# A decoder trunk on one core: thirty weight splits taken into the first feed-forward layer and kept in DRAM, layer norm additions on VectorE, conv taps loaded earlier and divided anew

## The chip, the core and the metric

The kernel runs on one core of a Trainium2 chip. A core has a matrix engine (TensorE, in the profile PE, with the loading of its weights as PEld), three engines for elementwise work (VectorE or DVE, ScalarE or ACT, GpSimd or POOL), and SyncE (SP), from whose queue nearly all transfers between DRAM and the on-chip memory are issued. Each engine works through its own instructions in order; semaphores tie them together. The metric is the device time of one execution in microseconds. Three runs of the kernel before gave 1237.91 to 1237.98, median 1237.97 us.

## The reference

The input is a sequence of 512 positions of 1024 features in float32. Two layers follow one another; each is a mixer and a feed-forward part, each with a scaled residual and a layer norm.

```python
for layer in range(DEPTH):                       # DEPTH = 2
    if layer % 2 == 0:                           # layer 0: state space group and attention group
        h = x @ mix_w_in[i] + mix_b_in[i]
        u, q, k, v = jnp.split(h, ...)
        mix = jnp.concatenate([s5_out, sb_out], axis=-1) @ mix_w_out[i] + mix_b_out[i]
    else:                                        # layer 1: conformer convolution
        mix = conformer_conv(x, conv_w_pw1[i], ...)
    x = layer_norm(DEEPNORM_ALPHA * x + mix, ln1_g[layer], ln1_b[layer])
    ffn = jnp.square(jax.nn.relu(x @ w1 + b1)) @ w2 + b2          # 1024 -> 4096 -> 1024
    x = layer_norm(DEEPNORM_ALPHA * x + ffn, ln2_g[layer], ln2_b[layer])

def conformer_conv(x, w_pw1, b_pw1, w_dw, b_dw, ln_g, ln_b, w_pw2, b_pw2):
    h = x @ w_pw1 + b_pw1                        # 1024 -> 2048
    val, gate = jnp.split(h, 2, axis=-1)
    h = val * jax.nn.sigmoid(gate)
    h = depthwise_causal_conv(h, w_dw) + b_dw    # 31 taps for each of 1024 channels
    h = jax.nn.silu(layer_norm(h, ln_g, ln_b))
    return h @ w_pw2 + b_pw2                     # 1024 -> 1024
```

## The kernel before

Features lie on the 128 partitions and positions along the free axis, so an activation is eight tiles of 128 x 512. All products are made at more than the precision of one pass: a matrix is split into a high part rounded to the type fp32r and the low rest, and a product is three passes, high by high, high by low and low by high (`gemm`, L199 to L208; its matmuls are on L207). Activations and weights are both split: `split` (L196) for activations, class `Weights` for weights.

**Weights.** `Weights` (L53 to L109) holds a list of units in the order of use. A unit is 8 x 128 rows by 128 columns, 512 KB in float32. `fetch` (L65) loads the chunk that a unit lies in, mostly 1 MB for two units, from SP's queue into one of two raw buffers. `_prep` (L77) then makes the parts: ACT casts the raw unit to the high part (L90) and DVE subtracts to get the low part (L91), both into one of eight slots in turn. `next` hands out the next unit and has the units up to five ahead prepared first. A slot is free again when PE has read its unit for the last time. Around a layer norm the splits can be held behind it by `fence`.

**Order of the work.** After the mixer of layer 0 come, in this order (chunks of the trace in brackets):

- `tail_norm_lead("a")`: the rest of the output product of the mixer ("tail", tiles tla, in two halves of 256 positions), the layer norm, and the first six products of the feed-forward part ("lead", tiles fl).
- The feed-forward part of layer 0 in four blocks of eight hidden tiles. `ffn1` makes the hidden tiles (f), `accum` adds their products to X (acf). For a block of eight, `accum` takes a unit for each of its eight columns. The last block's second product is the tail of the next step.
- The load of the 31 x 1024 conv taps in two pieces (L982), eight transposes on PE (L985) and their split on DVE (wdw, wdh, wdl).
- `tail_norm_lead("b")`: tail tlb, the layer norm and four lead products (pl), the first two tiles of the pointwise product of the convolution.
- The convolution. For each of the eight channel tiles `glu_tile` makes value and gate (pv, pg), their product hp and its split (hph, hpl); `taps_pe` gives some of the 31 taps to PE, each as a diagonal matrix that ACT makes in two parts (dh, dl; L1030 holds the matmuls, into cv); `taps_dve` gives two taps to ACT and the others to DVE (L339, two running sums cy and cz), and adds the sums and cv. `PE_TAPS` says how many taps of each tile PE takes, first for the whole tile or its first half, then for second halves. The last two tiles are worked in halves (tiles 6 and 7). Then comes the layer norm of the convolution for the first half, and for the second.
- `tail_norm_lead("d")`: the second pointwise product (tld), layer norm, six lead products for layer 1's feed-forward part (fl). `residual` rebuilds X from the split parts on POOL.
- The feed-forward part of layer 1 (f, g, h) and the final norm. Its weights follow the same unit order.

**The layer norm** (class `LN`) runs by halves. `add` sums the eight tiles as they come: the first six additions of a half on POOL, the last on DVE (L833). `colmean` (L841) is a product with a matrix of 1/1024 that gives the mean (mp...) and the variance (vp...). In `norm`, DVE subtracts the mean, ACT squares, POOL adds the squares of four tiles in a chain of three (L853), DVE adds those of the other four, and the variance product takes the two sums. `others` names products of PE that are issued ahead of the mean's and the variance's.

The order of instructions on an engine is made from the order in the code and a cost model of the framework, which lets later work move up where it judges earlier work not ready.

Of the kernel before, what the change touches and what calls it, by code (L numbers as in the profile page):

```python
# [16 lines left out]
P = 128  # L17
# [35 lines left out]
class Weights:  # L53


    def __init__(self, tc, ahead):
        self.tc, self.nc, self.ahead = tc, tc.nc, ahead
        self.slots, self.units, self.raw, self.urgent, self.fence, self.hold = [], [], None, True, None, False
        self.done, self.got, self.chunk, self.ready = 0, 0, {}, {}
# [17 lines left out]
    def _prep(self, n):  # L77
        nc = self.nc
        while self.done < min(n, len(self.units)):
            key, src, nk, ncol, off, width = self.units[self.done]  # L80
            self.fetch(self.done)
# [14 lines left out]
            self.done += 1  # L96

# [50 lines left out]
def kernel(ctx: ExitStack, tc: tile.TileContext, a: dict, out: bass.AP):  # L148
# [610 lines left out]
    def accum(nps, xk, name, ncol, first=True, cols=((0, T),)):  # L759
# [3 lines left out]
        for c0, c1 in cols:  # L763
            for j in range(KT):
# [7 lines left out]
                else:  # L772
                    tt(x, x, ps[:, c0:c1], ALU.add)

# [26 lines left out]
    units = units_of("mo", w_out, 4, 4, range(0, D, 256), 512)  # L801
    for layer in range(2):
        if layer:
            for j in range(0, D, 128):
                units += units_of("pw1", a["conv_w_pw1"][0], 0, 8, [j], 256)
                units += units_of("pw1", a["conv_w_pw1"][0], 0, 8, [D + j], 256)
            units += units_of("pw2", a["conv_w_pw2"][0], 0, 8, range(0, D, 128), 256)
        k0 = 0
        for nb in FFN_BLOCKS[layer]:
            units += units_of(f"f1{layer}", a["ffn_w1"][layer], 0, 8, range(k0 * P, (k0 + nb) * P, 128), 256)  # L810
            if layer == 0:
                units += units_of("f20", a["ffn_w2"][0], k0, nb, range(0, D, 1024 // nb), 256 if nb == 8 else 512)
# [9 lines left out]
    class LN:  # L822
# [5 lines left out]
        def add(self, j, ys, c0, c1):  # L828
# [3 lines left out]
            if j:  # L832
                (V if j == KT - 1 else G).tensor_tensor(self.s[c0], ys[0][:, c0:c1] if j == 1 else self.s[c0], ys[j][:, c0:c1], op=ALU.add)  # L833
# [10 lines left out]
        def norm(self, ys, c0, c1, others=(None, None)):  # L844
# [67 lines left out]
    class Lead:  # L912
# [35 lines left out]
    def ffn1(layer, bi, k0, nb, xs, fps, first=()):  # L948
        hs = []
        for i in range(nb):  # L950
# [12 lines left out]
            hs.append((hh, hl))  # L963
        return hs
# [7 lines left out]
    xs, first = tail_norm_lead(cat[4:8], "a", rb[0], ("ln1_g", 0), ("ln1_b", 0), LEAD, "fl0")  # L972
    k0 = 0
    for bi, nb in enumerate(FFN_BLOCKS[0]):
        hs = ffn1(0, bi, k0, nb, xs, nps, first if bi == 0 else ())
        if bi < len(FFN_BLOCKS[0]) - 1:
            accum(nps, hs, f"f0{bi}", 1024 // nb, bi == 0)
        k0 += nb
    wdw = hid.tile([P, KT, CONV], F32, tag="wdw", name="wdw")
    for f in range(2):  # L980
        wn = tmp(f"wn{f}")[:CONV]
        nc.sync.dma_start(wn, a["conv_w_dw"][0][:, f * T : (f + 1) * T])  # L982
        ps = stp(f"wd{f}")
        for i in range(4):
            PE.transpose(ps[:, i * 32 : i * 32 + CONV], wn[:, i * P : (i + 1) * P], ident[:CONV, :CONV])  # L985
        V.tensor_copy(wdw[:, 4 * f : 4 * f + 4, :], ps[:, :P].rearrange("p (i t) -> p i t", t=32)[:, :, :CONV])
    wdh = hid.tile([P, KT, CONV], F32R, tag="wdh", name="wdh")
    wdl = hid.tile([P, KT, CONV], F32, tag="wdl", name="wdl")
    V.tensor_copy(wdh, wdw)
# [211 lines left out]
```

## Time and profile before

| | us |
|---|---|
| median of three runs | 1237.97 |
| profiled execution | 1239.18 |
| its span (first to last instruction) | 1237.4 |
| PE busy | 1195.6 (97%) |
| DVE busy | 779.3 (63%) |
| ACT busy | 567.1 (46%) |
| POOL busy | 107.1 (9%) |

The page gives, for each engine, the time that its instructions cover, and a row of 40 digits, one for each fortieth of the span (31 us), with the busy share in tenths. PE's instructions overlap in the pipeline, so that a PE row of nines isn't proof that PE did as much as it can; the chain of waits and the gaps between PE's instructions say more. The chain that ended last runs through PE for 75% of the span, DVE for 16%, ACT 4%, DMA 3%. A row of a group reads: line, engine, operation, output and inputs by their names, shapes, count, then busy time in us and the mean of one in ns, then the idle time of the engine before them and who ended it.

### The profile page before, as it was taken

The numbers are of one execution on the slowest core, as the hardware profiler recorded it, in microseconds if no ns is written. First come the engines' busy times: TensorE is split into PE (matmuls) and PEld (weight loads), VectorE is DVE, ScalarE is ACT, GpSimd is POOL, SyncE is SP. The second block draws the span as 40 slices with busy tenths as digits, with TensorE's granted clock in tenths as the row PEclk, the third lists the DMA queues.
The fourth block names the chain that finished last, engine by engine and source line by source line (L and its number), as shares of the span: only waits on it lengthen the run. The fifth ranks groups of instructions, "written<-read, shape, count | busy, mean of one in ns | idle before, by whom it ended". The sixth has DMA issues, their size and how long they took to land.

```text
span 1237.4 us, 16678 instructions
## 1 busy us (share of the span) xinstructions
PE 1195.6 (97%) x6559; PEld 1015.3 (82%) x6559; DVE 779.3 (63%) x1321; ACT 567.1 (46%) x1020; POOL 107.1 (9%) x145
## 2 busy tenths in 40 slices
PE   9899999999999999999999999699899999999997
PEld 7776777789888888888998889689898888888885
DVE  8998774578633434434398999999853443434446
ACT  7736575635523324224255766876562332323230
POOL 1001100131000000000140011123400000000000
PEclk9999999999999999999999999889899999999999
DMA  8510141241533223333133121012052232423211
GB/s 206 162 37 20 35 119 52 85 137 42 163 102 102 80 90 102 102 102 98 43 103 103 35 69 35 1 48 90 33 172 69 85 119 68 134 68 105 86 51 68
DMA packets 111662, 105.93 MB, mean 86 GB/s; under 512 B 9378, under 2 KB 99746, under 8 KB 111584
## 3 DMA queue, kind: packets, MB, share of 16 engines
q1 hardware_dynamic: 111424, 104.84, 27.0%
q8 instruction: 51, 0.84, 0.3%
q14 instruction: 27, 0.22, 0.1%
q10 hardware_dynamic: 160, 0.03, 0.0%
HBM read 100.66 MB, written 4.19 MB: 85 GB/s over the span
## 4 chain that ended last, share of the span: by engine, by line
PE 75%; DVE 16%; ACT 4%; DMA 3%; issue 2%; POOL 1%; DVEq 0%; SPq 0%; ACTq 0%; POOLq 0%
PE f L207 23%; PE g L1131 12%; PE acf L207 11%; PE fl L207 4%; PE h L1115 3%; PE tld L207 3%; DVE cz L339 3%; PE tlb L207 2%; PE cv L1030 2%; DVE wlo L91 2%; DVE cy L339 2%; PE pl L207 1%; PE pv L207 1%; PE pg L207 1%; DVE X L339 1%
## 5 line engine op out<-in xcount | busy, mean ns | idle before, releaser
L90 ACT CAST whi<-raw 128x1024 fp32r<-128x1024 f32 x176 | 183.9, 1049 | 396.9 <-PE f L207 112.1
L91 DVE TENSOR_TENSOR wlo<-raw,whi 128x1024 fp32r<-128x1024 f32 x176 | 219.4, 1251 | 221.7 <-ACT whi L90 221.1
L1131 PE MATMUL g<-whi,hh 128*128 128x512 f32 x208 | 81.5, 392 | 0.0
L1131 PE MATMUL g<-wlo,hh 128*128 128x512 f32 x208 | 81.5, 392 | 0.0
L1131 PE MATMUL g<-whi,hl 128*128 128x512 f32 x208 | 81.4, 391 | 0.0
L207 PE MATMUL f<-xdh,whi 128*128 128x512 f32 x208 | 80.9, 389 | 0.0
L207 PE MATMUL f<-xah,whi 128*128 128x512 f32 x208 | 80.9, 389 | 0.0
L207 PE MATMUL f<-xal,whi 128*128 128x512 f32 x208 | 80.9, 389 | 0.0
L207 PE MATMUL f<-xdh,wlo 128*128 128x512 f32 x208 | 80.9, 389 | 0.0
L207 PE MATMUL f<-xdl,whi 128*128 128x512 f32 x208 | 80.9, 389 | 0.0
L207 PE MATMUL f<-xah,wlo 128*128 128x512 f32 x208 | 80.9, 389 | 0.0
L207 PE MATMUL acf<-hl,whi 128*128 128x512 f32 x192 | 75.2, 392 | 0.0
L207 PE MATMUL acf<-hh,whi 128*128 128x512 f32 x192 | 74.9, 390 | 0.0
L207 PE MATMUL acf<-hh,wlo 128*128 128x512 f32 x192 | 74.7, 389 | 0.0
L197 ACT CAST hh<-fr 128x512 fp32r<-128x512 f32 x64 | 39.7, 621 | 71.7 <-DVE fr L335 71.5
L198 DVE TENSOR_TENSOR hl<-fr,hh 128x512 fp32r<-128x512 f32 x64 | 44.2, 691 | 37.3 <-ACT hh L197 37.2
L339 DVE SCALAR_TENSOR_TENSOR cy<-hp,wdw,cy 128x512 f32<-128x512 f32 (+1 forms) x91 | 60.9, 678 | 0.1
L339 DVE SCALAR_TENSOR_TENSOR cz<-hp,wdw,cz 128x512 f32<-128x512 f32 (+1 forms) x86 | 59.9, 700 | 0.0
L1030 PE MATMUL cv<-hph,dh 128*128 128x256 f32 (+1 forms) x113 | 39.9, 353 | 10.0 <-ACT hph L197 8.3
L335 DVE TENSOR_TENSOR fr<-fr 128x512 f32<-128x512 f32 x64 | 43.8, 686 | 5.4 <-ACT fr L136 5.4
L1131 PEld LDWEIGHTS g<-whi,hl 128*128 128x128 f32 x208 | 39.1, 188 | 8.6
L1131 PEld LDWEIGHTS g<-wlo,hh 128*128 128x128 f32 x208 | 39.1, 188 | 8.6
(684 smaller groups left out, 3168.4 us busy)
## 6 DMA issues: line engine op xcount, KB each, us to landing
raw<-in_ffn_w_dram SPq DMA_DIRECT2D x48, 1024.0 KB, 5.4
raw<-in_ffn_w_dram SPq DMA_DIRECT2D x32, 512.0 KB, 3.5
raw<-in_conv_w_pw_dram SPq DMA_DIRECT2D x12, 1024.0 KB, 5.4
raw<-in_mix_w_in_dram SPq DMA_DIRECT2D x16, 512.0 KB, 4.0
xin<-in_x_dram SPq DMA_DIRECT2D x8, 256.0 KB, 4.1
raw<-in_s_w_glu_dram SPq DMA_DIRECT2D x4, 512.0 KB
raw<-in_mix_w_out_dram SPq DMA_DIRECT2D x4, 512.0 KB
raw<-in_mix_w_out_dram SPq DMA_DIRECT2D x2, 1024.0 KB
```

The lines of the kernel that those rows point to most:

```text
L90: i0 = nc.scalar.copy(hi, raw).ins
L91: i1 = nc.vector.tensor_sub(lo, raw, hi.bitcast(F32)).ins
L197: i0 = S.copy(hi, src).ins
L198: i1 = V.tensor_sub(lo, src, hi.bitcast(F32)).ins
L207: ins = PE.matmul(ps[:, c0:c1], u[:, k, ksl], v[:, c0:c1], start=start and k == 0 and i == 0, stop=stop and k == n - 1 and i == 2).ins
L335: V.tensor_tensor(o, x, y, op=op)
L339: V.scalar_tensor_tensor(o, x, s, y, op0=op0, op1=op1)
L1030: PE.matmul(cps[j][:, c0:c1], u, v[:, t + c0 : t + c1], start=t == 0 and i == 0, stop=t == n - 1 and i == 2)
L1115: PE.matmul(ps, u, v, start=k == 0 and i == 0, stop=k == nk - 1 and i == 2)
L1131: PE.matmul(pss[b], u, v[:, kk, :], start=k + kk == 0 and i == 0, stop=k + kk == nb - 1 and i == 2)
```

## The change

The change has six parts.

1. *Thirty units are split early and kept.* The 16 units of the first pointwise product (pw1), the 8 of the second (pw2) and the first 6 of layer 1's feed-forward part (f1l) get entries among the units of layer 0's feed-forward part: two after each group of four hidden tiles from tile 8 on, and two and four after the fourth and the eighth column of the first three `accum` calls. `keep` takes such a unit, split as any other, and writes both parts to DRAM from SP's queue, 512 KB each. In layer 1 these units are of the kind "split": `_prep` loads both parts from DRAM into the slot by POOL's queue, and makes no cast and no subtraction for them, and the fence doesn't hold them.
2. *The additions of the layer norms a, b, c and d* are all on DVE. The squares are added in four pairs on DVE, and the variance product takes four sources in place of two.
3. *The taps are loaded before block 1 of layer 0's feed-forward part*, with their transposes and split, and not before tail b.
4. *PE_TAPS* is changed; for the last two tiles the second half on PE is done for tile 7 before tile 6 (`TAIL`).
5. *The second halves of the first two of layer 1's lead products* are made together, input tile by input tile (`TOGETHER`).
6. *The residual's eight additions* in layer 1 are on DVE.

```diff
-PE_TAPS = ((5, 8, 10, 10, 9, 11, 17, 16), (10, 10, 10, 10, 10, 10, 13, 14))
+PE_TAPS = ((2, 6, 8, 9, 11, 14, 13, 14), (10, 10, 10, 10, 10, 10, 13, 8))
+TAIL = "P60 P70 V60 V70 G61 G71 N0 P71 P61 V61 V71 N1".split()
-GLU_FIRST = True
+TOGETHER = {'fl1': 2}
+LN_ON_V = "abcd"
+KEEP_FROM = 8
...
             key, src, nk, ncol, off, width = self.units[self.done]
+            if key[0] == "split":
+                pool, s = self.slots[self.done % len(self.slots)]
+                w = tuple(pool.tile([P, nk, ncol], F32R, tag=f"w{x}{s}", name=f"w{x}{self.done}", bufs=1) for x in ("hi", "lo"))
+                for x, d in zip(w, self.kept[key[1]]):
+                    nc.gpsimd.dma_start(x, d)
+                self.ready[self.done] = w
+                self.done += 1
+                continue
...
+    def keep(self, i):
+
+        w = self.next()
+        self.kept[i] = tuple(self.tc.dram_tile([P, *w[0].shape[1:]], F32, name=f"kept{x}{i}") for x in "hl")
+        for x, d in zip(w, self.kept[i]):
+            self.nc.sync.dma_start(d, x.bitcast(F32))
...
-                (V if j == KT - 1 else G).tensor_tensor(self.s[c0], ...)
+                (V if j == KT - 1 or self.n in LN_ON_V else G).tensor_tensor(self.s[c0], ...)
...
-            for j in (1, 2, 3):
-                G.tensor_tensor(sq[0], sq[0], sq[j], op=ALU.add)
-            tt(sq[4], sq[4], sq[5], ALU.add)
-            tt(sq[6], sq[6], sq[7], ALU.add)
-            tt(sq[4], sq[4], sq[6], ALU.add)
-            var = self.colmean([sq[0], sq[4]], c0, c1, "v", others[1])
+            for j in range(0, KT, 2):
+                tt(sq[j], sq[j], sq[j + 1], ALU.add)
+            var = self.colmean(sq[::2], c0, c1, "v", others[1])
...
         def finish(self):
             self.run(self.n - len(self.held))
-            for w, ps in self.held:
-                gemm(ps, w, slice(0, P), self.xs, *HALVES[1])
+            n, (c0, c1) = TOGETHER.get(self.name, 0), HALVES[1]
+            for k, (xh, xl) in enumerate(self.xs):
+                for (hi, lo), ps in self.held[:n]:
+                    for i, (u, v) in enumerate(((hi, xh), (hi, xl), (lo, xh))):
+                        PE.matmul(ps[:, c0:c1], u[:, k, :], v[:, c0:c1], start=k == 0 and i == 0, stop=k == KT - 1 and i == 2)
+            for w, ps in self.held[n:]:
+                gemm(ps, w, slice(0, P), self.xs, c0, c1)
...
     for bi, nb in enumerate(FFN_BLOCKS[0]):
+        if bi == 1:
+            taps()
         hs = ffn1(0, bi, k0, nb, xs, nps, first if bi == 0 else ())
...
-            G.tensor_tensor(X[j], xs[j][0].bitcast(F32), xs[j][1].bitcast(F32), op=ALU.add)
+            tt(X[j], xs[j][0].bitcast(F32), xs[j][1].bitcast(F32), ALU.add)
```

More of the change, by code (lines that the diff above doesn't have):

```diff
@@ L757, with accum @@
             glu()
-    def accum(nps, xk, name, ncol, first=True, cols=((0, T),)):
+    def accum(nps, xk, name, ncol, first=True, cols=((0, T),), keep=lambda j: ()):
         nj = ncol // P
@@ L773, in accum @@
                     tt(x, x, ps[:, c0:c1], ALU.add)
+                for k in keep(j):
+                    W.keep(k)
     accum(mm, cat[0:4], "mo", 256)
@@ L801 @@
     units = units_of("mo", w_out, 4, 4, range(0, D, 256), 512)
+    later = []
+    for j in range(0, D, 128):
+        later += units_of("pw1", a["conv_w_pw1"][0], 0, 8, [j], 256)
+        later += units_of("pw1", a["conv_w_pw1"][0], 0, 8, [D + j], 256)
+    later += units_of("pw2", a["conv_w_pw2"][0], 0, 8, range(0, D, 128), 256)
+    later += units_of("f1l", a["ffn_w1"][1], 0, 8, range(0, LEAD * P, 128), 256)
+    kept = [k for j in range(0, 16, 4) for k in (j, j + 2, j + 1, j + 3)] + list(range(16, 24 + LEAD))
+    keep_at, n = {}, 0
     for layer in range(2):
         if layer:
[L804 to L807, printed above, removed]
+            units += [(("split", i), None, 8, 128, 0, 0) for i in range(24 + LEAD)]
         k0 = 0
         for nb in FFN_BLOCKS[layer]:
-            units += units_of(f"f1{layer}", a["ffn_w1"][layer], 0, 8, range(k0 * P, (k0 + nb) * P, 128), 256)
+            for m in range(k0, k0 + nb, 4):
+                units += units_of(f"f1{layer}", a["ffn_w1"][layer], 0, 8, range(max(m, LEAD * layer) * P, min(m + 4, k0 + nb) * P, 128), 256)
+                if layer == 0 and m >= KEEP_FROM:
+                    keep_at["f", m + 3] = kept[n : n + 2]
+                    units += [later[i] for i in kept[n : n + 2]]
+                    n += 2
+            for j in range(0, KT, 4) if layer == 0 else ():
+                units += units_of("f20", a["ffn_w2"][0], k0, nb, range(j * P, (j + 4) * P, 128), 256)
+                if k0 + nb < 32:
+                    m = 4 if j else 2
+                    keep_at["a", k0, j + 3] = kept[n : n + m]
+                    units += [later[i] for i in kept[n : n + m]]
+                    n += m
             if layer == 0:
-                units += units_of("f20", a["ffn_w2"][0], k0, nb, range(0, D, 1024 // nb), 256 if nb == 8 else 512)
+                pass
             else:
@@ L963, in ffn1 @@
             hs.append((hh, hl))
+            for k in keep_at.get(("f", m), ()) if layer == 0 else ():
+                W.keep(k)
         return hs
@@ L1067 @@
             ln.add(j, [x and x[0] for x in acc], c0, c1)
[L1068 to L1069 removed]
+    for o in TAIL:
+        j, (c0, c1) = int(o[1]), HALVES[int(o[-1])]
+        if o[0] == "P":
             taps_pe(j, c0, c1)
[L1071 removed]
+        elif o[0] == "V":
             taps_dve(j, c0, c1)
             ln.add(j, [x and x[0] for x in acc], c0, c1)
[L1074 to L1089 removed]
+        elif o[0] == "G":
+            glu_tile(j, H, T)
+        else:
+            ys = [x[0] for x in acc]
+            r = ln.norm(ys, c0, c1)
+            cs_ = cs_ or new_x("cs")
+            for j in range(KT):
+                y = ys[j][:, c0:c1]
+                tt(y, y, r, ALU.mult)
+                act(y, y, AF.Silu, bias=pv("conv_ln_b", j), scale=pv("conv_ln_g", j))
+                done = split(cs_[j][0][:, c0:c1], cs_[j][1][:, c0:c1], y)
+                if c0 == 0 and j == FJ:
+                    W.fence = done
     W.ahead = AHEAD[0]
```

50 lines of the change are left out of this document (16 added, 34 removed).

## The prediction

> **What bounds the kernel now.** I read the page first, for the slices of busy time.
>
> ```profile
> PE   9899999999999999999999999699899999999997
> DVE  8998774578633434434398999999853443434446
> ```
>
> PE is nearly full everywhere, so only stretches in which PE waits can be shortened. DVE is full in slices 1 to 4 and again in 20 to 29, the tail of layer 0's feed-forward, the convolution and the tail behind it. The change acts there and in the feed-forward before it (slices 11 to 19, PE 9, DVE 3 to 5). Next I asked for busy time by stage, with the borders put at events of the chain of waits.
>
> ```profile
> 330.00:592.00 262.00, 262.00 (x1153) 216.07 (x1153) 106.45 (x121) 79.36 (x97) 0.00 (x0) 1.00 0.30 97
> 592.00:666.60 74.60, 73.37 (x598) 71.73 (x596) 49.59 (x97) 32.69 (x63) 17.90 (x18) 1.00 0.23 72
> 666.60:791.80 125.20, 116.56 (x644) 101.17 (x643) 124.80 (x198) 86.86 (x226) 13.44 (x11) 0.98 0.16 51
> 791.80:821.20 29.40, 26.90 (x164) 25.53 (x165) 26.98 (x71) 27.58 (x74) 3.19 (x4) 0.79 0.00 1
> 821.20:841.80 20.60, 18.11 (x140) 17.13 (x139) 19.61 (x40) 13.50 (x29) 8.20 (x9) 1.00 0.33 103
> 841.80:864.10 22.30, 22.26 (x181) 22.10 (x182) 21.19 (x42) 12.39 (x23) 8.85 (x9) 1.00 0.31 96
> 864.10:908.30 44.20, 39.68 (x296) 38.33 (x295) 35.98 (x51) 25.26 (x43) 14.77 (x12) 0.92 0.20 67
> ```
>
> The columns are the stage, its length, then busy time (and instructions) of PE, PEld, DVE, ACT and POOL, the granted clock, the DMA share and GB/s. I call the seven rows F (feed-forward), B (tail b), C (convolution), N0 and N1 (its layer norm for the two halves), T (tail d, second half) and L (tail's layer norm and the lead products). In C the DVE is busy 124.80 of 125.20 us: DVE is the bound, and PE ran ahead until it stood still once, as PE's own waits show:
>
> ```profile
> PE cv L1030 <- ACT hph L197: 8.3, 1, 8.3
> ```
>
> The chain of waits gives the order of events behind it.
>
> ```profile
> 782.08 0.40 DVE cy L339
> 784.06 0.33 DVE cy L335
> 792.58 0.85 PE mpc L841 x2
> 805.42 7.80 PE tld L207 x43
> 821.18 0.45 PE mpc L841 x2
> 824.80 1.67 DVE wlo L91
> 827.35 1.68 DVE wlo L91
> 831.22 1.13 DVE wlo L91
> 864.12 2.88 PE fl L207 x24
> 873.18 0.88 PE vpd L841 x4
> 885.79 2.93 DVE xdl L877 x2
> 888.76 19.57 PE fl L207 x146
> ```
>
> In it half 0's norm starts at 792.6 when the last tap is added, half 1's at 821.2; the chain of half 1 runs through three weight splits (wlo); from 880 to 888 it is xdl on DVE that PE's next products wait for.
>
> **The price of single instructions.** The timeline of DVE:
>
> ```profile
> 740.78 1.22 DVE L339 SCALAR_TENSOR_TENSOR cz<-hp,wdw,cz 128x512 f32<-128x512 f32 x1
> 743.25 0.74 DVE L339 SCALAR_TENSOR_TENSOR cy<-hp,wdw,cy 128x512 f32<-128x512 f32 x1
> 743.91 0.74 DVE L339 SCALAR_TENSOR_TENSOR cz<-hp,wdw,cz 128x512 f32<-128x512 f32 x1
> 753.82 1.23 DVE L91 TENSOR_TENSOR wlo<-raw,whi 128x1024 fp32r<-128x1024 f32 x1
> 754.96 1.24 DVE L339 SCALAR_TENSOR_TENSOR cz<-hp,wdw,cz 128x512 f32<-128x512 f32 x1
> ```
>
> From start to start a full tap costs 0.66 us (743.25 to 743.91), a split 1.14 (753.82 to 754.96). By the chain a half tap costs 0.40 and a 256-wide addition 0.33. Beside a POOL addition a tap lasts 1.22 instead of 0.74, 0.48 more. The groups by form, over 592 to 908 us, show the same beside the residual's POOL additions, 803 ns against 508:
>
> ```profile
> L877 DVE SCALAR_TENSOR_TENSOR xdl<-X,PV,xdh 128x256 fp32r<-128x256 f32 x16 | 12.1, 803 | 0.0
> L877 DVE SCALAR_TENSOR_TENSOR xbl<-X,PV,xbh 128x256 fp32r<-128x256 f32 x16 | 7.7, 508 | 0.2 <-ACT xbh L136 0.2
> ```
>
> The splits in stage C, ACT's half of a split over the whole run, the tap transposes, and a block of F:
>
> ```profile
> L91 DVE TENSOR_TENSOR wlo<-raw,whi 128x1024 fp32r<-128x1024 f32 x10 | 12.7, 1274 | 0.2 <-ACT whi L90 0.2
> ```
>
> ```profile
> L90 ACT CAST whi<-raw 128x1024 fp32r<-128x1024 f32 x176 | 183.9, 1049 | 396.9 <-PE f L207 112.1
> ```
>
> ```profile
> 595.32 0.43 PE L985 MATMUL wd<-ident,wn 31*128 31x31 f32 x4
> ```
>
> ```profile
> 373.73 43.52 PE f L207 x192
> 417.25 43.73 PE acf L207 x192
> ```
>
> A PE pass over 512 columns costs 43.52 / 192 = 0.23 us, over 256 columns 2.88 / 24 = 0.12; a tap or a k-tile is three passes.
>
> **Stage by stage.** The sum is made against the profiled execution: span 1237.4, time 1239.18 us; the median of the runs is 1237.97, 1.2 lower, and I take the difference off that median.
>
> *C, 125.2 us.* Removed from DVE: 10 splits x 1.14 = 11.4, and the slowing by 11 POOL additions, 11 x 0.48 = 5 (not all meet a tap squarely). Added: taps, since PE_TAPS falls from 53 to 50 for the six whole tiles and from 33 to 27 for the first halves, 3 x 0.66 + 6 x 0.40 = 4.4; the 11 additions themselves, 11 x 0.33 = 3.6. Net -8.4. PE's own work is 116.6 less 3 x 0.69 and 6 x 0.36 for the same taps, 112.3: still below DVE's 116.8, so DVE stays the bound and the stage can give 13 at most. Bounds -13 to +1, the latter if each of the 20 loads that replace the 10 splits slows one DVE instruction as POOL's additions did.
>
> *N0, 29.4 us.* Taps of the second halves on PE fall from 27 to 21: 6 x 0.40 more on DVE, and two more additions, 3.1 in all. DVE is idle for 2.4 us here, and ACT is full (27.58), with the taps' diagonals among its work, of which 12 go. I take +1.1; bounds -1.4 to +3.1.
>
> *N1, 20.6 us.* Three splits lie on the chain (1.67 + 1.68 + 1.13 = 4.5) and go; the variance product, two passes per source, gets four sources for two, 0.88 more by the vpd row, half of it before the last source is ready: -4.5 + 0.4, so I take -4.0. A POOL chain of three additions becomes one pairwise addition more on DVE. Bounds -7 (four splits of 1.14 and POOL's slowing of 2.4 gone from a DVE that is full) to 0.
>
> *T, 22.3 us.* PE is full; the variance product adds 0.9.
>
> *L, 44.2 us.* PE must do 288 lead passes at 0.12 = 34.6, a mean 0.44 and a variance 1.76: 36.8, with gaps 37.3. The rest of the 44.2 was the wait for xdl. From the last product to the last xdl DVE now takes 24.6 us (864.1 to 888.8); 16 x (803 - 508) ns = 4.7 of this goes with the residual's POOL additions, and the POOL chain before the variance too, so that it ends within the 19.5 us that PE has to do meanwhile (17.3 of first-half leads, the mean, the variance). The residual's eight additions come behind the lead on DVE, 8 x 0.6 at most, and row L shows 8 us of DVE idle for them. TOGETHER covers what is left of the wait. -6.9; bounds -7 to +4, the latter if the f1 loads come late.
>
> *B, 74.6 us.* PE is idle for 1.2 us, which goes with POOL's chains; the two variance products add 1.8, the transposes leave with 0.9: -0.3, bounds -1 to +4 (late loads again).
>
> *F, 262 us.* Thirty splits more: 34 us on DVE's 106 and 31 on ACT's 79, of 262: both hide under PE, and if splits were late, PE would stop for a unit of 24 passes, 5.4 us. The tap loads pass SP's queue behind raw loads and writes, and PE's transposes wait for them in order, with the first product of block 1 behind: +0.9, up to +5. The additions of LN "a" lie before F and change place as those of B do; I put them at nothing too, bounds -1.5 to +1.5.
>
> Sum: -8.4 + 1.1 - 4.0 + 0.9 - 6.9 - 0.3 + 0.9 = -16.7: **1237.97 - 16.7 = 1221.3 us.**
>
> **The transfers.** SP's queue gets 60 writes of 512 KB, and raw loads for the kept units.
>
> ```profile
> raw<-in_ffn_w_dram SPq DMA_DIRECT2D x48, 1024.0 KB, 5.4
> raw<-in_ffn_w_dram SPq DMA_DIRECT2D x32, 512.0 KB, 3.5
> out_dram<-X SPq DMA_DIRECT2D x8, 256.0 KB, 2.0
> ```
>
> A block of F is 43.52 + 43.73 = 87.25 us. It loads 8 MB now and with ten kept units 13 MB, and writes 10 MB: 24.1 million bytes, 276 GB/s. Row F shows a share of 0.30 at 97 GB/s, so full engines would move 323 GB/s (an estimate from that row): 85% is used. Reads then take 42 us of the block and leave 45 for 20 writes, 2.25 us each. A 512 KB write is bounded by 1.9 us (what the second 512 KB adds: 5.4 - 3.5) and 4.0 (twice the 256 KB row). I take 1.9, because writes follow one another in a queue: no wait. The Trainium skill, page "DMA: Bandwidth & Descriptors", section "Bandwidth", puts the HBM limit of a core at about 358 GB/s; by that there is more room, 23%, and the sum is the same, only the chance of the slower case less. A write waits for splits made up to five units earlier; behind it in SP's queue stand raw loads, two buffers ahead of ACT.
>
> Coming back, 60 loads are issued on POOL, in order, each waiting for its slot, that is for PE's last reader. Behind a waiting load stand only other loads, as all of POOL's additions of these stages move to DVE. No row shows a load on that queue, so it has 1.9 to 3.5 us, as SP's raw loads. The chain dates the first need:
>
> ```profile
> 619.26 2.73 PE tlb L207 x23
> 645.05 5.50 PE pl L207 x46
> ```
>
> The four units of pl take 15 to 28 us from 622 on, when tlb's first slot is free, and the second pair is needed at 645. The last four of pw2 take as long from 666.6 + 112.3 = 779 and are needed at 805.4 - 8.4 + 4 x 2.88 = 808.5. The six of f1 take 23 to 42 from T's first column, 841.8 - 11.3 + 2.9 = 833.4, and are needed between 853.7 and 868. I take 1.9, since loads can overlap in a queue: all in time. At 3.5 each the late ends above follow.
>
> Of POOL beside DVE, the Trainium skill, page "SBUF — State Buffer", section "Who interferes with whom", says that a DVE instruction with two SBUF inputs is held up by a POOL instruction that reads SBUF, not by one that only writes. By that, issuing loads would not slow taps, and C gives its 8.4; the first half of the rule agrees with the 0.48 us above, the second is in no row here.
>
> **Rivals.**
> - *PE alone is left* (0.10): DVE gains more than reckoned; C gives 13, N0 1.4, N1 7, L 7, B 1: 29 less, 1209. For it: the additions share no operand chain with the taps; against: the two norm chains remain, with nothing for PE to do.
> - *Given back* (0.12): POOL's loads slow DVE as its additions did (20 x 0.48 = 9.6 in C), or come late by as much: about 1231.
> - *Nothing* (0.04): both of these, near 1237.
> - *DMA becomes the bound of F* (0.11), the slower side: above 2.25 us per write PE waits for weights in three blocks; the gain of 16.7 is used up at 2.53 us (45 + 5.6 over 20). At 3.0, midway between the bounds: 3 x (60 - 45) = 45, less 16.7, so 1266. For it: two raw buffers in one queue with writes, 85% load. Against: PE has five units of lead, and slack in every block.
> - The forecast: 0.63, its own range 1213 to 1229.
>
> **How the numbers follow.** 1221.3 is the likeliest case. The range 1208 to 1236 reaches to the first rival's value and the given-back case; it leaves out the DMA-bound case (0.11), nothing (0.04) and about 0.05 of tails. A measurement of this kernel can tell about 0.2%, 2.5 us, from no change. Faster: 0.63 + 0.10 + 0.12 = 0.85; same 0.04; slower 0.11.
>
> **What would show it right or wrong.** In F: PE still 262 us of 262, DVE about 140, ACT about 110, DMA share 0.8 to 0.9 at 270 GB/s. If PE's waits name ACT whi or a raw DMA there, the last rival holds. In C: no L91 rows, no POOL additions, taps at 0.74 without 1.2 among them, the first mpc some 8 us earlier relative to the start of the taps. In N1: about 16.5 us from mpc to the last csl. In L: fl without a wait for xdl. POOL's queue should show loads that wait for PE, and PE none for them. Wrong: C as long as before, or idle PE in F.

## The result and the profile after

The changed kernel took 1218.74 us, median of four runs (1217.50 to 1219.79), beside 1237.94 us for four runs of the kernel before on the same chip: a ratio of 0.9846, 95% interval 0.9829 to 0.9863. The forecast was 1221.3. The profiled execution is the quickest of the four, 1217.5 us with a span of 1215.8, 21.6 less than before.

Busy time by stage in the kernel after, columns as in the prediction (stage, length, busy time of PE, PEld, DVE, ACT and POOL, granted clock, DMA share, GB/s); the rows are F, B, C, N0, N1 with T, and L:

```profile
330.50:593.40 262.90, 262.90 (x1155) 215.41 (x1154) 140.18 (x155) 110.09 (x137) 0.00 (x0) 1.00 0.78 265
593.40:667.20 73.80, 73.66 (x597) 72.62 (x597) 43.31 (x102) 19.29 (x41) 11.77 (x22) 1.00 0.46 155
667.20:783.30 116.10, 111.95 (x618) 97.22 (x616) 115.09 (x205) 72.82 (x199) 13.75 (x26) 1.00 0.39 134
783.30:812.90 29.60, 27.52 (x196) 26.21 (x197) 29.16 (x80) 21.53 (x59) 0.00 (x0) 0.95 0.01 2
812.90:848.90 36.00, 35.97 (x283) 35.19 (x283) 30.81 (x86) 19.14 (x44) 6.37 (x12) 1.00 0.51 174
848.90:885.60 36.70, 36.70 (x299) 36.43 (x298) 29.25 (x56) 22.86 (x41) 0.00 (x0) 1.00 0.14 48
```

PE is now full in F, B, N1 with T, and L; it waits only at the end of C and in N0. DVE is as full in C as it was (115.09 of 116.1), but C is 10 us shorter. POOL's busy time in C is no longer additions: its 26 instructions there are load issues. Pieces of the chain of waits of the same kernel, from the start of N1 on:

```profile
812.87 0.43 PE mpc L879 x2
...
837.35 11.51 PE tld L225 x96
848.86 2.88 PE fl L225 x24
...
868.28 5.76 PE fl L969 x48
874.04 11.52 PE fl L225 x96
```

From 812.87 on the chain is PE's work alone: no wlo stands in it, and fl follows fl without an xdl between. PE's longest wait from B to L, and POOL's longest waits, both of the kernel after (who waits, for whom, us in total, times, longest):

```profile
PE cv L1076 <- ACT hph L215: 4.0, 1, 4.0
```

```profile
POOL whi L88 <- PE tlb L225: 394.9, 8, 380.3
POOL whi L88 <- PE pv L225: 73.0, 6, 30.9
```

Loads wait for PE, as forecast, and PE waits for no load. The transfers (KB, median us from issue to landing) and the issues of the loads (ns, least, median, most):

```profile
kepth<-whi SPq DMA_DIRECT2D x30, 512.0 KB, 8.6
keptl<-wlo SPq DMA_DIRECT2D x30, 512.0 KB, 9.4
whi<-kepth POOLq DMA_DIRECT2D x30, 512.0 KB, 3.7
wlo<-keptl POOLq DMA_DIRECT2D x30, 512.0 KB, 4.5
```

```profile
L88 POOL DMA_DIRECT2D whi<-kepth x30: 527/530/674, 619.5 to 843.3; - x30
```

Below, stages are measured from PE's first instruction of one to its first of the next (F from the first f to the first tlb, then the first tlb, cv, mpc of the first half, mpc of the second, lead product fl, and f of layer 1). In us, each from the profiled run of its kernel:

| kernel | F | B | C | N0 | N1+T | L |
|---|---|---|---|---|---|---|
| before | 273.0 | 74.5 | 126.0 | 28.6 | 42.9 | 44.2 |
| after | 275.6 | 73.9 | 116.2 | 29.4 | 36.0 | 36.7 |
| no_keep | 275.5 | 74.4 | 130.0 | 31.8 | 36.8 | 37.1 |
| adds_only | 273.0 | 75.0 | 125.6 | 28.0 | 40.2 | 37.1 |
| keep_only | 276.5 | 85.7 | 118.2 | 45.3 | 39.5 | 45.6 |
| keep_only_early | 274.7 | 85.4 | 118.2 | 32.3 | 40.3 | 45.0 |
| adds_on_pool | 275.5 | 78.7 | 116.4 | 38.1 | 40.0 | 37.6 |
| adds_on_pool_early | 275.5 | 78.8 | 116.4 | 32.0 | 39.6 | 38.7 |
| sp_loads_adds_on_pool | 275.5 | 72.3 | 116.4 | 39.3 | 37.8 | 35.8 |
| sq_on_pool | 275.5 | 78.3 | 116.2 | 32.2 | 39.7 | 38.4 |
| old_taps_early | 275.5 | 73.9 | 116.7 | 33.3 | 39.1 | 36.7 |
| more_pe_taps | 275.5 | 73.8 | 116.4 | 32.0 | 36.0 | 36.7 |
| double_writes | 291.2 | 75.8 | 116.2 | 29.3 | 36.0 | 36.7 |
| two_sources | 275.5 | 72.1 | 116.2 | 32.5 | 35.1 | 35.8 |

What lies before F takes 317.1 to 319.8 us in these runs (318.9 before, 317.6 after), and what lies behind L 329.2 to 332.2. Each kernel's ratio is against the kernel before on its own chip (1238.07 to 1239.3 us), so ratios are compared, and 0.001 is 1.24 us.

### The profile page after: what moved, and what is told of

It is laid out like the page before. It is cut to its first block, busy times and chain, and to the rows that moved or that the text cites. A ratio compares the mean times of both kernels' runs of the same rounds, so it can differ in the third digit from the quotient of the medians.

```text
span 1215.8 us, 16751 instructions
## 1 busy us (share of the span) xinstructions
PE 1187.4 (98%) x6546; PEld 1007.5 (83%) x6546; DVE 786.9 (65%) x1400; ACT 557.1 (46%) x990; POOL 58.2 (5%) x125
## 4 chain that ended last, share of the span: by engine, by line
PE 83%; DVE 10%; ACT 4%; DMA 2%; issue 1%; POOL 0%; SPq 0%; DVEq 0%; POOLq 0%; ACTq 0%
PE f L225 23%; PE g L1175 12%; PE acf L225 11%; PE fl L225 5%; PE tld L225 4%; PE tlb L225 4%; PE h L1159 3%; PE cv L1076 2%; PE pv L225 2%; PE pg L225 2%; PE tla L225 2%; PE pl L225 2%; DVE cz L357 1%; PE acmo L225 1%; PE av L709 1%
## 5 line engine op out<-in xcount | busy, mean ns | idle before, releaser
L102 DVE TENSOR_TENSOR wlo<-raw,whi 128x1024 fp32r<-128x1024 f32 x176 | 213.4, 1224 | 199.5 <-ACT whi L101 198.7
L215 ACT CAST hh<-fr 128x512 fp32r<-128x512 f32 x64 | 39.7, 621 | 59.6 <-DVE fr L353 59.6
L216 DVE TENSOR_TENSOR hl<-fr,hh 128x512 fp32r<-128x512 f32 x64 | 44.1, 690 | 31.9 <-ACT hh L215 31.8
L357 DVE SCALAR_TENSOR_TENSOR cy<-hp,wdw,cy 128x512 f32<-128x512 f32 (+1 forms) x99 | 63.6, 654 | 0.2
L1175 PEld LDWEIGHTS g<-wlo,hh 128*128 128x128 f32 x208 | 39.1, 188 | 8.9
L1175 PEld LDWEIGHTS g<-whi,hl 128*128 128x128 f32 x208 | 39.1, 188 | 8.9
L1175 PEld LDWEIGHTS g<-whi,hh 128*128 128x128 f32 x208 | 39.1, 188 | 8.8
```

Source lines behind the costliest of these rows:

```text
L102: i1 = nc.vector.tensor_sub(lo, raw, hi.bitcast(F32)).ins
L215: i0 = S.copy(hi, src).ins
L216: i1 = V.tensor_sub(lo, src, hi.bitcast(F32)).ins
L357: V.scalar_tensor_tensor(o, x, s, y, op0=op0, op1=op1)
L1175: PE.matmul(pss[b], u, v[:, kk, :], start=k + kk == 0 and i == 0, stop=k + kk == nb - 1 and i == 2)
```

## The experiments

### Each part alone, and the change without it

**no_keep**: the kernel after without the kept units.

```diff
-            units += [(("split", i), None, 8, 128, 0, 0) for i in range(24 + LEAD)]
+            units += later
...
-                    keep_at["f", m + 3] = kept[n : n + 2]
-                    units += [later[i] for i in kept[n : n + 2]]
```

> The changed kernel without its first part: the thirty units are split in layer 1 by ACT and DVE again, nothing is written to DRAM or loaded back; the other five parts stay. Theory, that the splits' time on a full DVE is what is saved: the convolution stage grows by 10 splits x 1.14 = 11 us and more, as the new PE_TAPS leave DVE no room, the norm of its second half by 4, the feed-forward stage of layer 0 falls by its 2.6: 1231 to 1238 us, near the kernel before. Rival, that POOL's slowing of DVE is what is saved and the splits hide in gaps: at most 8 us over the changed kernel, under 1227.

Measured: 1235.75 us, 0.9972 (0.9960 to 0.9984). The kept units are worth 16 us in the finished change, and the total is in the theory's range. Its C, N0, N1 with T, and L:

```profile
667.60:797.60 130.00, 112.52 (x619) 97.39 (x617) 128.51 (x219) 82.72 (x209) 0.00 (x0) 0.95 0.16 50
797.60:829.40 31.80, 28.01 (x200) 26.35 (x200) 31.36 (x79) 25.41 (x63) 0.00 (x0) 0.95 0.03 6
829.40:866.20 36.80, 35.60 (x280) 34.84 (x280) 35.69 (x90) 24.27 (x49) 0.00 (x0) 1.00 0.35 111
866.20:903.20 37.00, 36.88 (x300) 36.41 (x299) 32.63 (x64) 23.34 (x42) 0.00 (x0) 1.00 0.18 60
```

Most of it lies in C, which is 13.8 us longer: DVE has the splits again (128.51 of 130.0), and PE's longest wait is at its end:

```profile
PE cv L1067 <- ACT hph L215: 17.5, 1, 17.5
```

N1 with T is only 0.8 longer, not 4. Four splits start between 824.6 and 829.0, all before the mean of the second half (829.3), so they fall on DVE in N0, which is 2.3 us longer at the same clock. F doesn't fall by 2.6 either.

**adds_only**: the kernel before with the sums, the squares and the residual on DVE as in the change, and nothing else of it.

```diff
-                (V if j == KT - 1 else G).tensor_tensor(self.s[c0], ...)
+                V.tensor_tensor(self.s[c0], ...)
...
-            G.tensor_tensor(X[j], xs[j][0].bitcast(F32), xs[j][1].bitcast(F32), op=ALU.add)
+            tt(X[j], xs[j][0].bitcast(F32), xs[j][1].bitcast(F32), ALU.add)
```

> The kernel before with the sums, squares and the residual on DVE and no other part. Theory: in the convolution 3.6 us are added and 5 of slowing go, so it hardly moves (-2 to 0); the stage of the lead products of layer 1 loses its wait for xdl, 5 to 7 us: 1229 to 1233 us, the gain being at the tail, not in the convolution. Rival of POOL's slowing: the convolution itself falls by 5 or more. A third view, that a full DVE takes all additions at their price: no gain, 1238 or more.

Measured: 1229.49 us, 0.9914 (0.9898 to 0.9930). The total is in the theory's range, and the gain is where it was expected: L gives 7.1 us and N1 with T 2.8, while C hardly moves. N1 with T is bound by PE here already, though three splits still stand on DVE in it:

```profile
820.20:860.40 40.20, 40.20 (x322) 39.67 (x321) 39.15 (x92) 25.18 (x51) 0.00 (x0) 1.00 0.33 106
```

**keep_only**: the kernel before with the kept units alone, written as an edit of the kernel after.

```diff
-LN_ON_V = "abcd"
+LN_ON_V = ""
...
-PE_TAPS = ((2, 6, 8, 9, 11, 14, 13, 14), (10, 10, 10, 10, 10, 10, 13, 8))
+PE_TAPS = ((5, 8, 10, 10, 9, 11, 17, 16), (10, 10, 10, 10, 10, 10, 13, 14))
```

(The squares, the residual, `TAIL`, `TOGETHER` and the place of the taps' load are put back too.)

> The kernel before with the first part alone: units kept, sums, squares and residual on POOL, old PE_TAPS, taps loaded before tail b, lead products one after the other. Theory: DVE's load in the convolution falls by 11.4 to 114, under PE's 116.6, so the stage is bound by PE and gives 8 to 9 us; the norm of the second half gives 4 to 6, the feed-forward part costs 2: 1224 to 1229 us. Rival of POOL's slowing: under 6 us, over 1232. If loads that wait behind POOL's additions come late: PE's waits name whi or wlo of the kept units.

Measured: 1261.81 us, 1.0176 (1.0159 to 1.0193). This expectation failed by over 30 us: the part that is worth 16 us in the change costs 22 by itself. C does give 7.8 us; B loses 11.2 and N0 16.6. PE's waits in it, 590 to 945 us:

```profile
PE vpc L879 <- POOL sqc L891: 7.9, 2, 4.1
PE tld L225 <- ACT csh L215: 5.7, 2, 4.8
PE pl L225 <- ACT xbh L154: 3.2, 2, 1.8
PE wd L1028 <- DMA wn<-in_conv_w_dw_dram: 3.1, 2, 2.1
```

PE doesn't wait for a kept load. It waits for the variance's squares on POOL and what hangs on the norm, and for the taps' load, which has its old place ahead of tail b and now stands behind the writes in SP's queue.

**adds_on_pool**: the kernel after with the sums and squares of the norms back on POOL (the residual stays on DVE).

```diff
-LN_ON_V = "abcd"
+LN_ON_V = ""
...
-            for j in range(0, KT, 2):
-                tt(sq[j], sq[j], sq[j + 1], ALU.add)
+            for j in (1, 2, 3):
+                G.tensor_tensor(sq[0], sq[0], sq[j], op=ALU.add)
```

> The changed kernel with the sums and the squares of the layer norms a to d back on POOL and two sources for the variance, all else as changed. Theory of the splits: in the convolution 11 additions leave DVE (3.6 us) and slow it by about 5, the chains of the norms get the POOL chain of three back, 1 to 2 us in each of the norms where PE has to wait: 3 to 8 us over the changed kernel, 1222 to 1227. And as POOL takes its queue in order, loads would wait behind additions that wait for DVE: if that decides, over 1230. Rival of POOL's slowing: 12 us or more of the 19 go, over 1230, with taps of 1.2 us in the convolution; if nothing but the splits mattered, no change.

Measured: 1237.75 us, 0.9984 (0.9975 to 0.9994): nearly the whole gain is gone, as in the case of over 1230 that the expectation allowed, and not its 1222 to 1227. C is as in the kernel after, so additions that slow taps are not where it went. B, N0 and N1 with T lost 4.8, 8.7 and 4.0.

The two parts aren't additive: -11 and +22 alone, -19 together with the new taps.

### What mixing loads and additions on POOL costs

**sq_on_pool**: the kernel after with only the squares' chain back on POOL.

```diff
-            for j in range(0, KT, 2):
-                tt(sq[j], sq[j], sq[j + 1], ALU.add)
-            var = self.colmean(sq[::2], c0, c1, "v", others[1])
+            for j in (1, 2, 3):
+                G.tensor_tensor(sq[0], sq[0], sq[j], op=ALU.add)
...
+            var = self.colmean([sq[0], sq[4]], c0, c1, "v", others[1])
```

> The kernel after (1218.74 us) with the squares' chain back on POOL (three additions on POOL and three on DVE for each half, two sources for the variance product instead of four); the sums stay on DVE. The order of ACT around the first half's norm is that of the kernel after. Theory (a variance product waits for a chain of three POOL additions that stands behind loads): PE waits 1.2 us at vpb, 2 to 4 at vpc and 1.3 at vpd, less 6 times 0.44 us for the shorter variance products: 1220 to 1224. Rival (the sums' additions alone are what POOL's queue cannot bear, the squares cost nothing): 1216 to 1219.

Measured: 1230.36 us, 0.9936 (0.9921 to 0.9951), 11 us over the kernel after and 6 over the expectation's upper end. POOL's queue in tail b of this kernel (start, length):

```profile
621.25 0.74 POOL L891 TENSOR_TENSOR sqb<-sqb,sqb 128x256 f32<-128x256 f32 x1 [0.31 <-ACT sqb L154]
622.96 0.57 POOL L88 DMA_DIRECT2D whi<-kepth  x1 [0.97 <-PE tlb L225]
...
625.81 0.53 POOL L88 DMA_DIRECT2D whi<-kepth  x1 [1.75 <-PE tlb L225]
...
628.66 0.53 POOL L88 DMA_DIRECT2D whi<-kepth  x1 [1.79 <-PE tlb L225]
...
632.58 0.75 POOL L891 TENSOR_TENSOR sqb<-sqb,sqb 128x256 f32<-128x256 f32 x1
...
634.96 0.75 POOL L891 TENSOR_TENSOR sqb<-sqb,sqb 128x256 f32<-128x256 f32 x1
...
650.00 2.41 POOL L891 TENSOR_TENSOR sqb<-sqb,sqb 128x256 f32<-128x256 f32 x3 [8.00 <-ACT sqb L154]
```

The first half's three additions last 14.5 us, since between them stand loads, each held until PE has read a slot for the last time; the second half's, with no load between, take 2.41. The mechanism was the expected one; its price was taken from PE's waits at the variance product alone, while what follows the norm (xbh, xdh) is late too (and 2.8 of the 11 us lie in N0, whose clock was 0.82 in this run):

```profile
PE fl L225 <- ACT xdh L154: 3.0, 1, 3.0
PE pl L225 <- ACT xbh L154: 2.8, 2, 2.1
```

**sp_loads_adds_on_pool**: as adds_on_pool, with the loads on SP's queue, so that POOL has additions only.

```diff
-                    nc.gpsimd.dma_start(x, d)
+                    nc.sync.dma_start(x.bitcast(F32), d)
```

> As adds_on_pool (1237.75 us), with the 60 loads of kept weights issued on SP's queue instead of POOL's, so that POOL has only additions. The order of ACT around the first half's norm is that of adds_on_pool, the late one. Theory (POOL's one queue makes the squares and sums stand behind loads that wait for PE): tail b gives back 4 to 5 us of its 78.7, the stretch behind the second half's mean 2 to 3 of its 40, N0 stays at 38: 1229 to 1232. Rival (the additions cost by themselves, wherever the loads are): 1236 to 1239. If loads on SP's queue come late behind raw loads: over 1239, with PE waiting for whi or wlo.

Measured: 1228.15 us, 0.9912 (0.9896 to 0.9929), 0.0072 or 9 us below adds_on_pool, and a little under what the theory gave. B, 78.7 us there, is 72.3, and PE has no wait left in it:

```profile
593.60:665.80 72.20, 71.91 (x589) 71.07 (x588) 39.16 (x88) 19.43 (x41) 13.77 (x18) 1.00 0.46 162
```

So it isn't the additions as such that cost in B, but their place behind loads. N0 stays at 39.3, so that has another cause.

### The order that the mixture is compiled to

In adds_on_pool, ACT makes the products that open the last second-half taps at another place than in the kernel after. First the kernel after, then adds_on_pool:

```profile
782.66 0.51 ACT L154 ACTIVATE cz<-hp,wdw 128x256 f32<-128x256 f32 x1
783.07 0.58 ACT L154 ACTIVATE cy<-hp,PV,wdw 128x256 f32<-128x256 f32 x1
```

```profile
812.10 0.49 ACT L154 ACTIVATE cz<-hp,wdw 128x256 f32<-128x256 f32 x1
812.50 0.59 ACT L154 ACTIVATE cy<-hp,PV,wdw 128x256 f32<-128x256 f32 x1
```

In the kernel after they start before the norm of the first half. In adds_on_pool three of the four start 22.5 us after it began (its mpc is at 789.6), behind all diagonals; the DVE's taps stand behind them.

**adds_on_pool_early** emits these four products ahead of the first half's norm:

```diff
-TAIL = "P60 P70 V60 V70 G61 G71 N0 P71 P61 V61 V71 N1".split()
+TAIL = "P60 P70 V60 V70 G61 G71 F61 F71 N0 P71 P61 V61 V71 N1".split()
...
+        elif o[0] == "F":
+            opened_early[j, c0] = open_taps(j, c0, c1)
```

> The kernel after with the layer norms' sums and squares back on POOL, as in the run adds_on_pool (1237.75 us), but with the four ACT products that open the last two tiles' taps of the second half (the 256-wide cy<-hp and cz<-hp) emitted ahead of the first half's norm instead of behind it. In adds_on_pool the compiled order of ACT has three of the four behind all diagonals, and N0 lasted 38.08 us instead of 29.42. Theory (that order, not POOL's own time, is what N0 lost): N0 falls by 7 to 9 us, the whole to 1228 to 1231. Rival (the late opening is a symptom and the second half's taps wait for something else, such as POOL's sum): 1235 to 1239.

Measured: 1232.29 us, 0.9951 (0.9936 to 0.9966). N0 falls by 6.1 us, less than the 7 to 9 expected, and the whole by 0.0033, 4.1 us: 1228 to 1231 missed by 1.3. The order explains most of what N0 lost. The 2.6 us that are left over the kernel after are no more than the clock can make: more_pe_taps below, which has the additions and the order of the kernel after, has an N0 of 32.0 us at the same granted clock, 0.84.

**keep_only_early** is keep_only with the same edit.

> The run keep_only (1261.81 us: the kernel before with only the kept weights added), with the four ACT products that open the last two tiles' taps of the second half emitted ahead of the first half's norm. In keep_only the compiled order of ACT has all four behind 37 diagonals, the DVE's taps behind those, and N0 lasts 45.25 us. Theory (two causes, the order and POOL's queue): N0 falls to 32 to 34, the whole to 1248 to 1251; still slower than the kernel before (1238 to 1239), by what the additions behind loads cost in tail b and L. Rival (loads behind additions alone, the order is a symptom): 1259 to 1263.

Measured: 1248.37 us, 1.0089 (1.0068 to 1.0110). N0 falls from 45.3 to 32.3, the whole by 0.0087, both as the theory had it. So of the 22 us of keep_only 11 are this order. Of what is left, B has the most, 10.9 us over the kernel before (85.4). Of what acts in B, this run differs from adds_on_pool (78.7) only in the place of the taps' load and transposes, so that 6.7 of the 10.9 go with that place and 4.2 with the rest, loads among additions on one queue. C gives 7.8 and N1 with T 2.7, N0 still loses 3.7.

### Taps

**old_taps_early** is the kernel after with the old `PE_TAPS` and the same early products, since with the old division the compiled order is the late one too.

> The kernel after (1218.74 us) with the division of taps of the kernel before (5, 8, 10, 10, 9, 11, 17, 16 on PE; second halves 13 and 14 for the last two), and the four opening ACT products of the second half emitted ahead of the first half's norm, since with this division the compiled order puts them behind all diagonals otherwise. Theory (DVE and PE are nearly level in C of the kernel after, 115.1 and 112.0 of 116.1): PE gets 4.2 us more there and becomes the bound, C 116.5 to 118; N0 gets 12 more diagonals on ACT and 2.2 us on PE, up to 3 longer: 1219.5 to 1224. Rival (DVE is still the bound, its 4.4 us fewer taps are a gain): 1214 to 1217.

Measured: 1225.70 us, 0.9901 (0.9886 to 0.9916), 1.7 over the theory's upper end: the division is worth 7 us, early products included. C hardly differs (116.7); N0 and N1 with T are 3.9 and 3.1 longer (beside more_pe_taps, whose clock in N0 is nearly the same, N0 is 1.3 longer):

```profile
784.40:817.70 33.30, 29.63 (x192) 27.61 (x193) 26.37 (x72) 28.64 (x83) 0.00 (x0) 0.85 0.08 29
817.70:856.80 39.10, 39.10 (x314) 38.63 (x313) 31.92 (x88) 19.11 (x44) 6.33 (x12) 1.00 0.49 162
```

In N0 PE has 81 tap passes in place of 62 and gets through 95 passes of tld in place of 123; the 28 others follow in N1 with T, where PE is full (39.10 of 39.10).

**more_pe_taps**: three more taps on PE in whole tiles, to fill its wait of 4 us at the end of C.

```diff
-PE_TAPS = ((2, 6, 8, 9, 11, 14, 13, 14), (10, 10, 10, 10, 10, 10, 13, 8))
+PE_TAPS = ((2, 6, 9, 10, 12, 14, 13, 14), (10, 10, 10, 10, 10, 10, 13, 8))
```

> The kernel after with three more of the convolution's taps on PE (tiles 2, 3 and 4: 9, 10 and 12 of 31 instead of 8, 9 and 11). In the kernel after PE stands 4.2 us at the end of the convolution before the last tile's cv, and DVE is full. Theory (DVE is the bound of C, PE has 4 us to spare): DVE loses 3 x 0.66 = 2.0 us, PE gains 3 x 0.69 = 2.1, C falls by 1.5 to 2: 1216.5 to 1217.5. Rival (both engines are level, the wait only moves): 1218 to 1220.

Measured: 1219.91 us, 0.9847 (0.9829 to 0.9865): no difference, as the rival had it. PE's wait for hph at cv is gone, and PE waits for the last sum instead:

```profile
PE mpc L879 <- DVE sc L871: 2.4, 1, 2.4
```

The two engines are level, and moving taps only moves the wait.

### The writes

**double_writes** writes each kept part twice.

```diff
             self.nc.sync.dma_start(d, x.bitcast(F32))
+        for n, x in zip("hl", w):
+            self.nc.sync.dma_start(self.tc.dram_tile([P, *x.shape[1:]], F32, name=f"again{n}{i}"), x.bitcast(F32))
```

> The kernel after with each kept half unit written to DRAM twice, to two places: 120 writes of 512 KB in the feed-forward of layer 0 instead of 60; everything is computed. In the kernel after that stretch has a DMA share of 0.78 at 265 GB/s, so full engines would move 340 GB/s. Theory (bandwidth is the limit, PE waits once it is used up): a block of 87.6 us must move 24.1 + 10.5 = 34.6 million bytes, 102 us at 340 GB/s, so 14 us more in each of three blocks: 1254 to 1266, with PE's waits ending at ACT whi or a raw DMA. Rival (each write costs 1.9 us of the engines beside the loads, as the prediction had it): about 31 us per block, 1305 to 1315. Rival (writes are hidden, the raw loads go first): 1217 to 1224.

Measured: 1237.69 us, 0.9995 (0.9981 to 1.0009), 18 us over the kernel after. All three expectations missed; it lies between the first and the third. Three stretches of F, then its last 18 us with the first 10 of tail b, and PE's longest waits in F (the share adds up packets' times, and passes 1 where they overlap):

```profile
330.50:417.00 86.50, 86.50 (x384) 70.83 (x383) 44.24 (x51) 35.25 (x50) 0.00 (x0) 1.00 0.93 330
417.00:505.00 88.00, 84.43 (x362) 68.47 (x361) 40.77 (x45) 30.65 (x36) 0.00 (x0) 0.98 0.95 349
505.00:592.00 87.00, 79.85 (x336) 63.97 (x335) 39.65 (x44) 30.79 (x36) 0.00 (x0) 0.96 0.94 339
592.00:620.00 28.00, 28.00 (x165) 24.87 (x164) 16.74 (x22) 12.87 (x17) 0.00 (x0) 1.00 1.05 391
```

```profile
PE f L227 <- ACT whi L101: 9.2, 2, 6.1
```

PE's waits end at ACT's cast, as expected, and ACT in turn waits 77 us in F for raw loads (49.0 and 28.3 for the two tensors). So the transfers are late, and on average they run at about the 340 GB/s that were computed. That isn't the rate of full engines, though. In fortieths of the second stretch (2.2 us each, busy tenths, then GB/s):

```profile
DMA  9999199999999917999999999999990699999999
GB/s 373 410 404 382 61 240 249 422 415 382 400 419 401 363 52 184 317 421 417 370 390 421 419 423 412 371 400 412 395 335 31 167 309 422 419 381 390 419 402 365
```

Most stand near 400, and the average has three dips in it. In one of them SP's queue issues nothing from 437.74 to 448.82; in the whole stretch its raw loads wait 35.9 us for DVE to be done with a raw buffer. How much of the loss is bandwidth and how much these two buffers isn't separated. PE loses nothing in the first stretch, since units are prepared ahead, and the last writes delay nobody: they run on into tail b at 391 GB/s. The estimate of three times 14 us left both ends out, and it gave ten kept units to each of three blocks, as the prediction did, where the code gives 6, 10, 10 and 4 to the four.

### A variance product of two sources

**two_sources** adds the squares once more on DVE in the norms a, b and d.

```diff
+            if self.n in "abd":
+                for j in (0, 4):
+                    tt(sq[j], sq[j], sq[j + 2], ALU.add)
...
+            var = self.colmean(sq[::step], c0, c1, "v", others[1])
```

> The kernel after with two more DVE additions of squares in the layer norms a, b and d, so that their variance products have two sources instead of four; c keeps four. Theory (PE is the bound in these tails, a variance product of four sources costs 1.76 us there and of two 0.88): six halves give back 0.88 each, 5.3 in all: 1213 to 1215 beside 1218.7. Rival (the added level of additions, 0.4 us, makes PE wait for the variance's last source instead): 1217 to 1220.

Measured: 1217.43 us, 0.9832 (0.9817 to 0.9847), not told apart from the kernel after with 0.9846. Its stages B, N0, N1 with T, and L:

```profile
592.80:664.90 72.10, 71.96 (x590) 71.12 (x589) 44.59 (x106) 19.43 (x41) 11.78 (x22) 1.00 0.48 158
...
781.10:813.60 32.50, 30.51 (x196) 29.38 (x196) 29.16 (x80) 21.66 (x59) 0.00 (x0) 0.81 0.00 1
813.60:848.70 35.10, 35.07 (x279) 34.39 (x278) 31.39 (x89) 19.15 (x44) 6.34 (x12) 1.00 0.51 181
848.70:884.60 35.90, 35.90 (x297) 35.74 (x296) 29.50 (x57) 22.59 (x41) 0.00 (x0) 1.00 0.15 46
```

B, T and L give 1.7, 0.9 and 0.9 us, as priced at 0.88 for each half of b and d, and no new wait appears in them; for the norm a no gain stands out (317.3 us up to F beside 317.6). In N0 the same 196 instructions of PE took 32.5 us at a granted clock of 0.81, beside 29.6 at 0.95 in the profiled run of the kernel after; that hides the gain in the whole. So the total lies where the rival had it, but not by the rival's wait.

## Why the prediction was right, point by point

The sum of -16.7 us came out as -19.2 by the medians. C, L and B were right in cause and about right in size, L with a reservation. N0 agrees by luck, and N1 with T and F don't agree. The profiled execution, from which the stages are read, gained 2.4 more than the medians. In the total the misses partly cancel: N1 with T gave 3.9 more than forecast, F 1.7 less.

**C** (-8.4, measured -9.7). DVE was and stayed the bound. Removing the splits is what gave it: without the kept units C is 13.8 longer. That POOL's loads don't slow taps is shown in the kernel after, where 26 load issues ran beside them:

```profile
L357 DVE SCALAR_TENSOR_TENSOR cz<-hp,wdw,cz x76: 493/746/762, 684.2 to 783.9; 128x512 f32<-128x512 f32 x60, 128x256 f32<-128x256 f32 x16
```

No tap of the 76 took over 762 ns, where taps beside additions took 1.22 us before. The prediction drew this from the Trainium skill, page "SBUF — State Buffer", section "Who interferes with whom": a DVE instruction with two SBUF inputs contends with a POOL instruction that reads SBUF, not with one that only writes it. The trace agrees with the second half too, for which there was no row before. Moving the additions off POOL was worth little in C: with them on POOL again C is 116.4, and with them alone moved to DVE 125.6 beside 126.0. The forecast had 5 us less for the slowing and 3.6 more for the additions. The 5 us were about right: in C of the kernel before, six full taps, three half ones and one split are lengthened, by 5.0 us together. Most of what DVE saves there it spends on the eleven additions; of the net 1.4 forecast the stage shows 0.2 and 0.4.

**L** (-6.9, measured -7.5) is right in size, and its wait for xdl is gone: adds_only alone gives 7.1, without `TOGETHER`, which is left with 0.4 at most. But "The rest of the 44.2 was the wait for xdl" holds only in part. PE was idle for 4.5 us of the row L (39.68 busy of 44.20). PE's busy time falls as well, to 36.70, though it has 0.9 us more of variance: its granted clock was 0.92 there and is 1.00 now. In the kernel before, the clock is 0.50 from 886.1 to 892.8, where the wait for xdl ends.

**B** (-0.3, measured -0.6) agrees. **N0** (+1.1, measured +0.8) agrees only because the clocks differ: 0.79 in the row before, 0.95 in the row after. At 0.81 the same instructions take 32.5 us (two_sources), which is 3.9 over the kernel before and beyond the bound of +3.1.

**N1 with T** (-4.0 + 0.9, measured -7.0) is the step that failed: "Three splits lie on the chain (1.67 + 1.68 + 1.13 = 4.5) and go". They did go, and from the second mpc to the end of the last csl it is 16.3 us in place of 21.1, as forecast. But the stage isn't as long as this chain makes it. In adds_only three splits are still there, the chain takes 17.6, and PE is full all the same. What counts is PE's work, and T was not a fixed piece of it, as the prediction took it. PE does 46 more passes of tld in N0 (123 in place of 77), 46 x 0.12 = 5.5 us less for N1 with T; its 2.5 us of idle time in N1 (18.11 busy of 20.60) go; and eight more variance passes cost 1.8. That makes -6.2 of the -7.0. By the runs, 2.8 come with the additions on DVE (adds_only) and 3.1 with the division of taps (old_taps_early). The prediction counted the taps that leave PE in N0 only as a cost on DVE.

**F** (+0.9, measured +2.6). There is no PE wait over 0.11 us in it. Neither writes nor splits cause the surplus: no_keep has the same 275.5 us. About 0.8 is the eight transposes, as forecast. The other 1.8 lies in the passes of acf, 576 in all, which start 231.4 ns after one another on average in place of 228.3. For the block that the prediction shows with 43.73 us:

```profile
417.35 44.32 PE acf L225 x192
```

They are as slow in no_keep (231.3), which writes nothing, and in keep_only_early (231.1), which loads the taps later, and not in adds_only (228.3). Why stays open. The additions of norm a were put at nothing; what lies before F is 1.3 shorter, but in more_pe_taps, the same there, it is only 0.1 shorter, so nothing is shown.

**Transfers.** A write was put at 1.9 us of the engines, between bounds of 1.9 and 4.0, with 2.53 as the point where the gain is gone. At a share of 0.95 double_writes moved 349 GB/s, so 512 KB cost 1.5 us there, and the value was a little high. The slower rival didn't come, but what it feared exists: 31 million bytes more used up the gain. The limit of 358 GB/s that the prediction weighed isn't the limit of this core: 391 GB/s stands in a row above. The Trainium skill, page "HBM Reference", section "Specifications (TRN2)", says that a core alone measures well above its share of a pair, about 425 GB/s; the row agrees in direction.

**The loads.** "I take 1.9, since loads can overlap in a queue": they landed in 3.7 and 4.5 us, above the upper bound of 3.5, and were in time all the same, since PE waits for none.

**Given back** (0.12) didn't happen, and the runs show how near it was. The clause that stood against it, "Behind a waiting load stand only other loads", is worth up to 11 us for the squares alone (sq_on_pool), and about 9 for squares and sums when the loads leave POOL's queue instead (sp_loads_adds_on_pool).

Left open: why the order of ACT is compiled late in keep_only, adds_on_pool and with the old taps is not shown, only what it costs; the place of the taps' load, `TAIL` and `TOGETHER` weren't tried alone in the kernel after.

## What to carry to other kernels

A queue that issues loads with waits in it should have nothing else: three additions on POOL took 14.5 us in place of 2.4 between loads that wait for slots, and taking the loads off that queue gave back 9 us. Kept weights that gain 16 us in the whole change cost 22 without the rest of it, 11 of them by the order of one engine's instructions and some 7 by one small load left behind the new writes. When work leaves the chain that seems to bound a stage, count what the matrix engine still has to do in it before crediting the chain's time; here a stage that was forecast by its chain was bound by PE, and its size came out wrong by 3.9 us. And compare the order of instructions of two kernels, and their granted clocks, before explaining a difference by a part's price.

## What the runs showed of the hardware

- A load of 512 KB from POOL's queue into an fp32r tile keeps POOL for 0.53 us and lands in 3.7 to 4.5 us (medians for the two halves).
- Loads and writes together reached 349 GB/s over 88 us, dips included, and 391 GB/s over 28 us; in single slices of 2.2 us up to 423.
- In the kernel before, a tap on DVE beside a POOL addition took 1.22 us in place of 0.74; beside the 26 load issues of the kernel after none was lengthened.
- The same 196 PE instructions of N0 took 29.6 us at a granted clock of 0.95 and 32.5 at 0.81, in two kernels that differ only outside the stage; both times PE had stood 4 us shortly before. In the first the clock was 0.50 from 783.3 to 786.5 only, in the second from 779.6 to 786.3 and again from 793.2 to 799.9. What decides between them isn't shown by these runs.
